# Seven block products in the first feed-forward's way down of a decoder layer

## The chip, the cores and the metric

The kernel runs on one core of one Trainium2 chip. A core has TensorE (PE in the profile; its weight loads are PEld), VectorE (DVE), ScalarE (ACT), GpSimd (POOL) and SyncE (SP), which work on their own queues and wait for each other by semaphores; 16 DMA engines move data between HBM, SBUF and back. The metric is the device time of one execution in microseconds, as the median of the runs; less is better.

## The reference, cut to what matters

One hybrid decoder layer in float32, 1024 tokens of width 1024: a SwiGLU feed-forward, a mixer of stick-breaking attention and a Mamba-2 SSD side by side, a cross-attention to 256 memory tokens, and a second SwiGLU feed-forward, each between two RMS norms. The change is in the first feed-forward's second product.

```python
D_MODEL = 1024
SEQ = 1024
D_FF = 2816

def swiglu(h, w_gu, w_down):
    gu = h @ w_gu
    g, u = jnp.split(gu, 2, axis=-1)
    return (jax.nn.silu(g) * u) @ w_down

def reference(...):
    h = x
    for l in range(DEPTH):
        f = swiglu(rmsnorm(h, ffn1_pre_g[l]), ffn1_w_gu[l], ffn1_w_down[l])
        h = h + 0.5 * rmsnorm(f, ffn1_post_g[l])
        m = hybrid_mixer(rmsnorm(h, mix_pre_g[l]), w_in[l], ...)
        h = h + rmsnorm(m, mix_post_g[l])
        c = memory_cross_attention(rmsnorm(h, xa_pre_g[l]), rmsnorm(mem, mem_g[l]), ...)
        h = h + rmsnorm(c, xa_post_g[l])
        f = swiglu(rmsnorm(h, ffn2_pre_g[l]), ffn2_w_gu[l], ffn2_w_down[l])
        h = h + 0.5 * rmsnorm(f, ffn2_post_g[l])
    return h
```

## The kernel before, in words

**Products.** A float32 product is made of three matmuls in a 32-bit matmul type. Each operand is split into hi, a rounded copy (`split`, L248, an ACT copy), and lo, the remainder (L250, a VectorE subtract); `mm3` issues hi x hi, hi x lo and lo x hi into one PSUM bank. All matmuls pass line 137. Activations are kept transposed: width on the 128 partitions, tokens along a row, in two halves `hh` of H = 512 tokens.

**Seven products for eight.** A product of matrices cut into 2 x 2 blocks needs eight block products, or seven, if sums and differences of the blocks are formed first and the results are combined afterwards. The up phases of both feed-forwards (`seven`) and the second feed-forward's way down (`down7`, called by `down_rows`) are written so. The first one's way down (`down1`) takes all eight: 22 k-tiles of 128, 8 output tiles, 2 halves.

**The first feed-forward.** `ffn1` runs `up_phase`, which for each of 22 tiles f of the inner width makes two activation tiles (one for each half), stores them to HBM (`store`, on ACT's queue) as `act_d`, and then `down1`. `down1` goes in three groups of blocks (0 to 2, 3 and 4, then 5 to 10, where a block is two k-tiles), each for both output halves `dh` and both token halves; between groups the partial sums go from PSUM into `F` (copies L972, sums L477). The last group runs token half 0 first, and `post(0)`, the norm behind the feed-forward of half 0 with its residual and the next norm's scale, runs beside the products of half 1. `post(1)` runs beside the start of the SSD. `post` takes the sums of squares (`sumsq`), two small products that gather them and spread them over the partitions (`rms_cols`, `rms_rows`), then for each of 8 tiles: scale (L388), residual (L392), the hi copy (L399), the lo part (L404) and the next sum of squares (L349, L350). `resid` loads the residual on POOL's queue.

**The second feed-forward's way down.** In `down7` the seven products are `m` = 0 to 6, each over 11 block pairs `j`. For a step (m, j) `fetch` loads the blocks that don't stay in SBUF, forms the weights' sum on VectorE (L1025), splits weights and activations, and `take` keeps some five steps ready ahead. The activations' sums were formed at the end of the up phase (`pair_sums`, or `act_sums`, which reloads the first pairs from HBM) and stored as `xs_d`. Two of the four weight blocks stay in SBUF (`stay`), in the tiles of the normed input that the up phase has done with. In the last product the last four pairs are taken together, bank by bank.

**Order.** TensorE's order is that of the program text. `self.clock` counts the estimated time of TensorE's instructions, 0.422 ns a column; `self.later` holds pairs of such a time and a function, and `run_later` issues what is due after each matmul. Instructions issued that way keep their order on their engines (`kp`). Others are placed by the scheduler.

**Prepared weights.** `prepare_all` splits 58 weight tiles of later stages during the up phase and the way down: each tile in two pieces, a load, a copy (L209), a subtract (L214) and two stores to HBM on SP's queue. Later stages then load hi and lo (L180) and split nothing. Its pieces use SBUF tiles in three places, among them the ninth buffers of `xl0` and `xl1`.

Of the kernel before, what the change touches and what calls it, by code (L numbers as in the profile page):

```python
# [46 lines left out]
class Kern:  # L47
    def __init__(self, nc, tc, ap):
        self.nc, self.tc, self.ap = nc, tc, ap
        self.uid = 0  # L50
        self.clock = 0.0
        self.prev = None
        self.floating = None
        self.pins = []
        self.later = []
        self.inlater = False
        self.more = False
# [131 lines left out]
    def prepare(self, tiles, sp, t0, step):  # L189
# [3 lines left out]
        work, out = [], []  # L193
        for src in tiles:
            hl = tuple(self.tc.dram_tile([P, KT, P], F32R, name=self.nm(n)) for n in ("dwhi", "dwlo"))
            out.append(hl)
            work += [(src, hl, slice(4 * i, 4 * i + 4)) for i in range(2)]
        pools = ((self.fp, "acc0"), (self.fp, "acc1")), ((self.fp, "rpost"), (self.tp, "dg")), ((sp, "bh"), (sp, "bl"))
        raws, his, los = {}, {}, {}

        def load(n):
            pool, tag = ((sp, "braw"), (sp, "braw"), (self.xp, "xl0"), (self.xp, "xl1"))[n % 4]
            raws[n] = self.t(pool, [P, 4, P], F32, tag, bufs=2 if pool is sp else KT + 1)
            self.kp(nc.sync.dma_start(out=raws[n], in_=work[n][0][:, work[n][2], :]))

        def high(n):
            pool, tag = pools[n % 3][0]
            his[n] = self.t(pool, [P, 4, P], F32R, tag)
            self.kp(nc.scalar.copy(his[n], raws[n]))  # L209

        def low(n):
            pool, tag = pools[n % 3][1]
            los[n] = self.t(pool, [P, 4, P], F32R, tag)
            self.kp(nc.vector.tensor_tensor(out=los[n], in0=raws[n], in1=his[n].bitcast(F32), op=ALU.subtract))  # L214

        def store(n):
            for d, x in zip(work[n][1], (his.pop(n), los.pop(n))):
# [288 lines left out]
    def ffn1(self, wgu, wdn, gpre, gpost, gnext, begin):  # L506
# [3 lines left out]
        rw, dnp = st.enter_context(self.pools("ff", [], ["r"]))  # L510
        self.fp = rw
        act_d, bank, load = self.ffn(dnp, rw)
        with tc.tile_pool(name=self.nm("up"), bufs=1, reuse_waits="tile") as sp, \
                tc.tile_pool(name=self.nm("ub"), bufs=1, reuse_waits="tile") as sp2:
            self.up_phase(sp, sp2, wgu, gpre, act_d, bank, load, None, (3, 2, 3), rw, begin)
        f1 = st.enter_context(tc.tile_pool(name=self.nm("d1"), bufs=1, reuse_waits="tile", side="right"))
        with tc.tile_pool(name=self.nm("dl"), bufs=1, reuse_waits="tile") as sp, \
                tc.tile_pool(name=self.nm("d0"), bufs=1, reuse_waits="tile", side="right") as f0:
            self.new_F(f0, f1)
            self.down1(sp, wdn, act_d, bank, load, gpost, gnext)  # L520
# [16 lines left out]
    def up_phase(self, sp, sp2, wgu, gpre, act_d, bank, load, plain, sizes, rw=None, begin=None):  # L537
# [4 lines left out]
        ftp = sp if begin else rw  # L542
# [24 lines left out]
        spare = [] if begin else [self.xl(hh, F32) for hh in range(2)]  # L567

        def store(f, hh, t):
# [3 lines left out]
            if stored[f // 2] == 4 and not begin:  # L573
                later_sums.append(f // 2)

        def act_sums(j, t0):
# [4 lines left out]
            def load(n):  # L581
                if n == "a22":
                    x[n] = self.t(self.tp, [P, H], F32, "dg", bufs=1)
                else:
                    x[n] = self.t(rw, [P, H], F32, "cb", bufs=3)
# [25 lines left out]
        def pair_sums(f, even, odd):  # L611
# [9 lines left out]
            def fresh(n, a, b, op):  # L621
                combine(n, self.t(rw, [P, H], F32, "cb", bufs=3), a, b, op)
# [132 lines left out]
        def seven(f):  # L755
# [40 lines left out]
            if begin or f < 4:  # L796
# [81 lines left out]
    def down1(self, sp, wdn, act_d, bank, load, gpost, gnext):  # L878

        nc = self.nc
        NB = NFF // 2
        dx = [self.t(sp, [P, 2, H], F32R, "dx", bufs=2) for _ in range(2)]
        ends = range(NB - 6, NB)
        groups = [(bs, dh, hh) for bs in (range(0, 3), range(3, 5)) for dh in range(2) for hh in range(2)]
        groups += [(ends, dh, hh) for hh in range(2) for dh in range(2)]
        steps = [(n, b) for n, (bs, _, _) in enumerate(groups) for b in bs]

        def keys(n, b):  # L890
            bs, dh, hh = groups[n]
            return ("a", b, hh), ("w", b, dh, hh if bs is ends else 0)

        uses = {}
        for i, x in enumerate(steps):
            for k in keys(*x):
                uses.setdefault(k, []).append(i)

        spots = {("a", 0, 0): (1, 4), ("a", 1, 0): (1, 6), ("a", 2, 0): (0, 4), ("a", 0, 1): (0, 6), ("a", 1, 1): (1, 0), ("a", 2, 1): (1, 2)}
        for hh in range(2):  # L900
            spots.update({("a", ends[j], hh): (1, k) for j, k in enumerate((4, 6, 0, 2))})

        free, rings = {}, {"a": [], "w": []}
        for k in uses:
            ring = rings[k[0]]
            if k in spots:
                owners = [x for x in uses if spots.get(x) == spots[k] and uses[x][0] < uses[k][0]]
                free[k] = uses[owners[-1]][-1] + 1 if owners else 0
            else:
                free[k] = uses[ring[-4]][-1] + 1 if len(ring) > 3 else 0  # L910
                ring.append(k)
        at, count = {}, [0] * len(steps)
        for k in reversed(list(uses)):
            due = max(uses[k][0] - 2, 0)
# [1455 lines left out]
```

## Time and profile before

| | us |
|---|---|
| median of 3 runs | 2669.76 |
| lowest, highest run | 2667.02, 2671.39 |
| profiled execution | 2668.63 |
| its span, first to last instruction | 2666.4 |
| VectorE busy | 1912.6 |
| ScalarE busy | 1274.6 |
| first up phase, from the span's start to its last product | 452.45 |

The mean granted clock of TensorE is 0.995. In the page, a line of groups reads: line, engine, operation, output <- inputs, count | busy us, mean ns of one | idle time of the engine just before, and who ended it. "x12" behind a timeline's row counts equal instructions in a run. `hl`, `dx`, `whi`, `wlo`, `blk` are buffers of split operands, `dn` and `mm` are PSUM banks.

### The profile page before, as it was taken

How to read it: one execution, taken by the hardware profiler on the slowest of the kernel's cores; microseconds unless marked ns; L12 is line 12 of the kernel's file. 1: busy time of each engine (PE TensorE's matmuls, PEld its weight loads, DVE VectorE, ACT ScalarE, POOL GpSimd, SP SyncE). 2: the span in 40 equal slices, each digit the busy share in tenths (PEclk: the TensorE clock that was granted, in tenths of full speed). 3: DMA queues.
4: the chain of work that ended last, by engine and by line, in shares of the span. 5: the costliest groups of instructions: out<-in, count | busy, mean ns of one | idle time of the engine just before them, and what ended most of it. 6: DMA issues, size and time to landing. Idle time of an engine off the chain costs nothing. (4 is left out here: it accounts for less than half of the span.)

```text
span 2666.4 us, 36628 instructions
## 1 busy us (share of the span) xinstructions
PE 2615.6 (98%) x12970; PEld 2176.7 (82%) x12970; DVE 1912.6 (72%) x2907; ACT 1274.6 (48%) x2263; POOL 591.9 (22%) x676
## 2 busy tenths in 40 slices
PE   9999999999999999999999999999999899999999
PEld 7788888878877778888888897787878688888887
DVE  6888887456568775677777877775557788777777
ACT  7444444444345564555555555354555433333553
POOL 2555553000100000111111110101012655552000
PEclk9999999999999999999999999999999999999999
DMA  5578888984632215444444556544257353236554
GB/s 208 195 267 284 277 284 279 342 288 161 214 127 80 80 64 194 126 122 112 103 121 127 166 164 219 185 150 143 95 177 265 119 166 126 88 107 222 189 168 152
DMA packets 198535, 463.58 MB, mean 174 GB/s; under 512 B 24144, under 2 KB 32720, under 8 KB 198352
## 3 DMA queue, kind: packets, MB, share of 16 engines
q1 hardware_dynamic: 157888, 366.59, 41.4%
q0 software_dynamic: 22464, 61.88, 7.7%
q10 hardware_dynamic: 18000, 32.78, 3.3%
q8 instruction: 102, 1.67, 0.3%
q14 instruction: 81, 0.66, 0.1%
HBM read 313.04 MB, written 127.14 MB: 165 GB/s over the span
## 5 line engine op out<-in xcount | busy, mean ns | idle before, releaser
L137 PE MATMUL mm<-xh,whi 128*128 128x512 f32 x1364 | 536.5, 404 | 7.7 <-ACT xh L248 2.5
L137 PE MATMUL mm<-xh,wlo 128*128 128x512 f32 x1316 | 504.1, 392 | 0.6 <-ACT xh L248 0.6
L137 PE MATMUL mm<-xl,whi 128*128 128x512 f32 (+1 forms) x1258 | 490.0, 390 | 3.2 <-DVE xl L250 3.0
L137 PEld LDWEIGHTS mm<-xh,whi 128*128 128x128 f32 x1364 | 256.8, 188 | 53.3 <-issue 3.8
L137 PEld LDWEIGHTS mm<-xh,wlo 128*128 128x128 f32 x1316 | 247.5, 188 | 54.9 <-ACT xh L248 1.0
L137 PEld LDWEIGHTS mm<-xl,whi 128*128 128x128 f32 x1258 | 237.7, 189 | 37.3 <-DVE xl L250 4.0
L1763 DVE TENSOR_TENSOR_SCAN nb<-nb,begin 128x128 f32<-128x128 f32 (+7 forms) x128 | 171.8, 1353 | 57.8 <-ACT nb L1759 56.8
L1759 ACT ACTIVATE nb<-z,scale 128x128 f32<-128x128 f32 (+2 forms) x192 | 107.9, 581 | 80.0 <-PE z L137 79.8
L248 ACT CAST whi<-wraw 128x1024 fp32r<-128x1024 f32 (+1 forms) x102 | 93.1, 914 | 94.0 <-PE mm L137 66.8
L137 PE MATMUL dn<-xh,wlo 128*128 128x512 f32 x396 | 136.0, 390 | 1.7 <-DMA wlo<-dwlo 1.7
L250 DVE TENSOR_TENSOR wlo<-wraw,whi 128x1024 fp32r<-128x1024 f32 x70 | 85.5, 1221 | 59.1 <-ACT whi L248 58.8
L137 PE MATMUL dn<-xh,whi 128*128 128x512 f32 x356 | 122.8, 391 | 0.0
L1780 POOL DMA_DIRECT2D mix<-sq x64 | 52.8, 826 | 227.2 <-DVE sq L1778 168.6
L710 POOL TENSOR_TENSOR wc<-wraw,raw 128x512 f32<-128x512 f32 x58 | 84.3, 1454 | 74.8 <-DVE whi L250 26.7
L710 POOL TENSOR_TENSOR wc<-raw,wraw 128x512 f32<-128x512 f32 x56 | 83.0, 1481 | 60.9 <-DVE wlo L250 21.4
L795 POOL TENSOR_TENSOR ft<-ft,e 128x512 f32<-128x512 f32 x38 | 62.3, 1640 | 133.5 <-DVE e L794 54.9
L250 DVE TENSOR_TENSOR atl<-tr,ath 128x512 fp32r<-128x512 f32 (+1 forms) x108 | 67.9, 632 | 31.7 <-ACT ath L248 31.2
L632 ACT ACTIVATE ft<-ft 128x512 f32<-128x512 f32 x88 | 55.4, 631 | 73.4 <-DVE ft L631 72.6
L137 PE MATMUL dn<-xh,blk 128*128 128x512 f32 x280 | 90.3, 389 | 0.0
L137 PEld LDWEIGHTS dn<-xh,wlo 128*128 128x128 f32 x396 | 74.4, 188 | 17.9 <-DMA wlo<-dwlo 2.2
L248 ACT CAST whi<-wc 128x512 fp32r<-128x512 f32 x81 | 50.4, 622 | 76.8 <-PE dn L137 30.2
L248 ACT CAST ath<-tr 128x512 fp32r<-128x512 f32 (+1 forms) x108 | 58.9, 546 | 56.5 <-PE tr L140 51.7
(543 smaller groups left out, 6658.1 us busy)
## 6 DMA issues: line engine op xcount, KB each, us to landing
whi<-dwhi SPq DMA_DIRECT2D x78, 512.0 KB, 3.3
wlo<-dwlo SPq DMA_DIRECT2D x78, 512.0 KB, 4.3
wraw<-in_w_gu SPq DMA_DIRECT2D x44, 512.0 KB, 4.0
raw<-in_w_gu SPq DMA_DIRECT2D x38, 512.0 KB, 4.2
act<-ft ACTq DMA_DIRECT2D x70, 256.0 KB, 2.8
h<-F POOLq DMA_DIRECT2D x40, 256.0 KB, 3.0
xl<-h POOLq DMA_DIRECT2D x40, 256.0 KB, 5.2
dwhi<-acc SPq DMA_DIRECT2D x39, 256.0 KB, 5.2
```

Source lines behind the costliest of these rows:

```text
L137: self._pe(self.nc.tensor.matmul(out, lhsT, rhs, start=start, stop=stop, skip_group_check=self.more), cost)
L248: self.kp(self.nc.scalar.copy(hi, src))
L250: self.nc.vector.tensor_tensor(out=lo, in0=src, in1=hi.bitcast(F32), op=ALU.subtract)
L632: nc.scalar.activation(t, t, AF.Silu)
L710: nc.gpsimd.tensor_tensor(out=t, in0=a, in1=b, op=op)
L795: nc.gpsimd.tensor_tensor(out=t1, in0=t1, in1=e, op=ALU.mult)
L1759: nc.scalar.activation(nb[:, s0:s1], z[:, 0:n], AF.Sigmoid, scale=sc[:, i : i + 1])
L1763: nc.vector.tensor_tensor_scan(out=nb[:, 0:Wd][:, ::-1], data0=nb[:, 0:Wd][:, ::-1], data1=begin[:, S - Wd : S][:, ::-1], initial=0.0, op0 ...
L1780: nc.gpsimd.dma_start(out=self.mix_d[p][a * 64 : a * 64 + 64, csl], in_=o, accum_op=ALU.add)
```

## The change

`down1` is rewritten on top of `down7`, which gets a switch: with `rows=False` the weights' tiles are the stationary operand and the activations the moving one, so the result comes transposed, and the blocks of the result are found at other places of `F`. The first up phase forms the activations' sums as the second does: for the last nine pairs from the tiles that are still in SBUF, for the first two by a reload. It gets a pool of its own for that (`up_pool`: six tiles `ft`, three `cb`), which stays open through the way down; four tiles of `F` and the weights' sums then use it. Only 44 weight tiles are prepared in the first feed-forward, at a slower step; the eight `out` tiles are prepared in attention and the six `gu2` tiles in cross-attention, each with a small pool of its own. A prepared piece now uses one of two places, and its four steps are issued at times of their own.

```diff
-    def prepare(self, tiles, sp, t0, step):
+    def prepare(self, names, raw, pairs, t0, step, slow=None):
...
-        def event(n):
-
-            for f, m in ((low, n - 1), (store, n - 2), (high, n), (load, n + 2)):
-                if 0 <= m < len(work):
-                    f(m)
-
-        self.later += [(t0 + step * n, lambda n=n: event(n)) for n in range(-2, len(work) + 2)]
-        return out
+        t = t0
+        for n in range(len(work)):
+            for f, m, dt in ((high, n, 0), (low, n, 1200), (load, n + 2, 2400), (store, n, 3000)):
+                if m < len(work):
+                    self.later.append((t + dt, lambda f=f, m=m: f(m)))
+            t += step if slow is None or t < slow[0] else slow[1]
+        for n in range(2):
+            self.later.append((t0 - 8000 + 1000 * n, lambda n=n: load(n)))
+
+    def prep_pool(self, sp):
+
+        return (sp, "braw"), [((sp, "bh", 2), (sp, "bl", 2)) for _ in range(2)]
 
     def prepare_all(self, sp):
-        ap = self.ap
         names = [("ssd", i) for i in [*range(6), *range(12, 26)]] + [("qkv", i) for i in range(24)]
-        names += [("out", i) for i in range(8, 16)] + [("gu2", i) for i in range(2 * PLAIN)]
-        self.ready = dict(zip(names, self.prepare([ap["w_" + n][i] for n, i in names], sp, 95000, 3870)))
+        pairs = [((self.fp, "acc0", None), (self.fp, "acc1", None)), ((sp, "bh", None), (sp, "bl", None))]
+        self.prepare(names, (sp, "braw"), pairs, 95000, 4700, (418000, 6200))
...
+        self.up_pool = st.enter_context(tc.tile_pool(name=self.nm("uf"), bufs=1, reuse_waits="tile", side="right"))
...
-            self.up_phase(sp, sp2, wgu, gpre, act_d, bank, load, None, (3, 2, 3), rw, begin)
+            xs_d = self.up_phase(sp, sp2, wgu, gpre, act_d, bank, load, None, (6, 2, 3), rw, begin)
...
-            if stored[f // 2] == 4 and not begin:
+            if stored[f // 2] == 4 and f < 4:
                 later_sums.append(f // 2)
...
-            if begin or f < 4:
+            if f < 4:
                 store(f, 0, t0)
                 store(f, 1, t1)
                 return
...
-    def down1(self, sp, wdn, act_d, bank, load, gpost, gnext):
...
+    def down1(self, sp, wdn, act_d, xs_d, gpost, gnext):
+
+        place = self.blocks_down(sp)
+        H_ = [[self.t(self.xp, [P, H], F32, f"xh{hh}{d}") for d in range(KT)] for hh in range(2)]
+        L_ = [[self.xl(hh, F32) for d in range(KT)] for hh in range(2)]
+        stay = {(1, 1): L_[0][4:8] + H_[0][4:8] + H_[0][0:3], (0, 0): H_[1][4:8] + L_[1][4:8] + H_[1][0:3]}
+        accs = []
+
+        def squares(hh, d, tag):
+            if d == 0:
+                accs[:] = self.new_accs(tag)
+            self.sumsq(accs, d, self.F[hh][d])
+
+        def at(t, f, *args):
+            self.later.append((self.clock + t, lambda: f(*args)))
+
+        def finish(m, i):
+            if m == 3:
+                self.run_later(float("inf"))
+                for d in range(4):
+                    at(5000 + 4000 * d, squares, 0, d, "acc0")
+                self.resid(0, 2000, 16000)
+            elif m == 4:
+                self.run_later(float("inf"))
+                for d in range(4, 8):
+                    squares(0, d, "acc0")
+                self.XH[0] = [self.t(self.xp, [P, H], F32R, f"xh0{d}") for d in range(KT)]
+                self.post(0, gpost, self.C[0], gnext, step=2600, accs=accs[:])
+            elif m == 5:
+                for d in range(4):
+                    at(2000 + 4000 * d, squares, 1, d, "bh")
+                self.resid(1, 2000, 14000)
+            elif m == 6:
+                squares(1, 4 + i, "bh")
+
+        self.down7(sp, wdn, act_d, xs_d, place, stay, finish, False)
         self.flush(0)
-        self.post(1, gpost, self.C[1], gnext, step=2000, accs=accs, at=(6500, 9000, 10000), tail=(7500, 10500))
+        self.XH[1] = [self.t(self.xp, [P, H], F32R, f"xh1{d}") for d in range(KT)]
+        self.post(1, gpost, self.C[1], gnext, step=2000, accs=accs[:], at=(6500, 9000, 10000), tail=(7500, 10500))
...
-    def down7(self, sp, wdn, act_d, xs_d, place, stay, finish):
+    def down7(self, sp, wdn, act_d, xs_d, place, stay, finish, rows=True):
...
+                        a, b = (x, w) if rows else (w, x)
                         self.mm3(
-                            banks[i], [(x[:, 0, c], x[:, 1, c], w[:, 0], w[:, 1])], first, j + jj == NB - 1
+                            banks[i], [(a[:, 0, c], a[:, 1, c], b[:, 0], b[:, 1])], first, j + jj == NB - 1
                         )
...
-                    (C11, C12), (C21, C22) = (self.F[hh][2 * i : 2 * i + 2] for hh in range(2))
+                    (C11, C12), (C21, C22) = (
+                        self.F[hh][2 * i : 2 * i + 2] if rows else self.F[hh][i : i + 5 : 4] for hh in range(2)
+                    )
...
+            self.prepare([("out", i) for i in range(8, 16)], *self.prep_pool(wsp), self.clock + 30000, 20000)
...
+                    self.prepare([("gu2", i) for i in range(2 * PLAIN)], *self.prep_pool(wsp), self.clock + 9000, 7000)
```

More of the change, by code (lines that the diff above doesn't have):

```diff
@@ L566, in up_phase @@
         xs_d, stored, later_sums, held = {}, [0] * (NFF // 2), [], []
-        spare = [] if begin else [self.xl(hh, F32) for hh in range(2)]
+        spare = [self.xl(hh, F32) for hh in range(2)]
         def store(f, hh, t):
@@ L876, in up_phase, with blocks_down @@
         return xs_d
[L878 to L883 removed]
+    def blocks_down(self, sp):
         dx = [self.t(sp, [P, 2, H], F32R, "dx", bufs=2) for _ in range(2)]
[L885 to L914, printed above, removed]
[L915 to L921 removed]
+        nblk = [0]
         def place():
```

114 lines of the change are left out of this document (25 added, 89 removed).

## The prediction, made before the changed kernel ran

> **What bounds the kernel now.** I read the page first: engines, then the slices.
>
> ```profile
> span 2666.4 us, 36628 instructions
> PE 2615.6 (98%) x12970; PEld 2176.7 (82%) x12970; DVE 1912.6 (72%) x2907; ACT 1274.6 (48%) x2263; POOL 591.9 (22%) x676
> PEclk9999999999999999999999999999999999999999
> ```
>
> TensorE is busy for 98% of the span at full clock, so it looks like the bound. But matmuls overlap and their ends are modelled, so the price of one is its distance from the next. The chain of waits and TensorE's timeline at both ends of the first way down give it:
>
> ```profile
> 2424.23 138.72 PE dn L137 x612
> ...
> 452.45 0.39 PE L137 MATMUL mm<-xh,whi 128*128 128x512 f32 x1
> ...
> 698.65 0.39 PE L137 MATMUL mm<-xh,whi 128*128 128x512 f32 x1
> ```
>
> 612 matmuls in 138.72 us are 0.2267 us each (the recorded 0.39 is a latency). At 452.45 the last product of the up phase ends and down1 begins; at 698.65 the SSD's first projection begins: 246.2 us. down1 has 22 k-tiles x 8 x 2 halves x 3 = 1056 matmuls, 239.4 us at that pace; the rest is norm products and waits. The waits of TensorE for sums into F, by the view of who waited for whom:
>
> ```profile
> PE mm L137 <- DVE F L477: 1.0, 1, 1.0
> PE dn L137 <- DVE F L477: 0.7, 1, 0.7
> ...
> PE mm L137 <- ACT F L972: 0.5, 1, 0.5
> ```
>
> 2.2 us at changes of accumulation group. So this stage is TensorE's, and a matmul less there is 0.2267 us less. The table of stretches shows how near the others are (length; busy us and count of PE, PEld, DVE, ACT, POOL; clock; DMA share; GB/s):
>
> ```profile
> 180.00:270.00 90.00, 90.00 (x399) 74.55 (x398) 73.60 (x93) 43.08 (x75) 52.74 (x34) 1.00 0.82 271
> 270.00:360.00 90.00, 90.00 (x399) 74.55 (x398) 74.28 (x97) 41.60 (x73) 54.16 (x34) 1.00 0.83 284
> 360.00:450.00 90.00, 90.00 (x399) 74.55 (x398) 69.72 (x91) 41.83 (x76) 42.14 (x27) 1.00 0.80 267
> 450.00:517.00 67.00, 66.46 (x294) 54.72 (x293) 34.17 (x53) 32.41 (x60) 3.81 (x5) 1.00 0.97 349
> 637.00:667.00 30.00, 30.00 (x142) 25.12 (x141) 24.00 (x41) 15.43 (x27) 3.24 (x6) 1.00 0.38 140
> 2448.00:2478.00 30.00, 30.00 (x134) 24.83 (x133) 26.98 (x47) 18.54 (x35) 2.63 (x5) 1.00 0.74 238
> 2478.00:2508.00 30.00, 30.00 (x134) 24.84 (x133) 21.04 (x33) 14.66 (x27) 0.00 (x0) 1.00 0.60 195
> 2598.00:2628.00 30.00, 29.73 (x140) 24.47 (x139) 24.62 (x43) 14.80 (x31) 3.24 (x6) 1.00 0.68 228
> ```
>
> The last three rows are the second feed-forward's way down, which already runs seven products through down7: TensorE loses 0.3 us there, with VectorE at 70 to 90%. VectorE is the next in line, so I price it by its starts:
>
> ```profile
> 2468.57 1.89 DVE L1025 TENSOR_TENSOR wc<-xl,xh 128x512 f32<-128x512 f32 x3
> 2470.38 0.69 DVE L250 TENSOR_TENSOR hl<-wraw,hl 128x512 fp32r<-128x512 f32 x1
> ...
> 2643.29 1.41 DVE L1149 SCALAR_TENSOR_TENSOR F<-F,st,mm 128x512 f32<-128x512 f32 x2 [0.32 <-PE mm L140]
> 2644.61 0.75 DVE L1144 SCALAR_TENSOR_TENSOR F<-F,rh,xl 128x512 f32<-128x512 f32 x1
> ```
>
> Three starts from 2468.57 to 2470.38: 0.60 us for a tensor_tensor of 128x512. Two of the three-operand form from 2643.29 to 2644.61: 0.66.
>
> **The change, part by part.** *TensorE.* Seven products of 11 block pairs, 4 banks, 3 matmuls: 924 for 1056. The two programs' TensorE instructions differ by just these 132; which operand is stationary changes neither count nor shape. 132 x 0.2267 = **-29.9 us**. The old groups' waits go too: **-2.2** (the cover is the other down7, which loses 0.3).
>
> *VectorE in the new way down.* The program's order lists 300 instructions there: 148 subtracts for splits, 55 weight sums, 24 sums into F, 20 subtracts of prepared weights, the rest norms and the last activation sums. At 0.60 that is 181 us under 924 x 0.2267 = 209.5, so on average it is hidden. It isn't spread evenly. post(0) now stands on products six and seven alone. From its first instruction that reads the gathered row to the subtract of the last block pair, VectorE has 68 instructions in order: 16 of the 0.66 form, 52 of 0.60: 41.9 us. They can't begin earlier than the row: post issues it 12.0 us after the fifth product by the kernel's count of 0.216 us a matmul, 12.6 real. The norm products, from the timeline:
>
> ```profile
> 705.69 0.95 PE L137 MATMUL ms<-small,bh 128*128 128x1 f32 x8
> 706.50 0.48 PE L137 MATMUL mm<-xl,whi 128*128 128x512 f32 x1
> ...
> 709.10 1.05 PE L137 MATMUL ms<-ident,cpost 128*128 128x128 f32 x8
> 709.90 0.48 PE L137 MATMUL mm<-xh,whi 128*128 128x512 f32 x1
> ...
> L248 ACT CAST whi<-wraw 128x512 fp32r<-128x512 f32 x15 | 9.3, 621 | 13.2 <-PE mm L137 5.8 <-PE dn L137 4.0 <-DMA wraw<-in_w_dn 3.3
> ```
>
> take 0.8 each (start of the matmul behind less their own): 14.2. With about 0.9 (an estimate: a matmul's latency of some 0.3 and an ACT copy of 0.6, as in the last row) to the row in SBUF: 15.1. So the last subtract ends at 15.1 + 41.9 = 57.0 us or later. TensorE wants it after product six (11 x 2.72 + 1.6 = 31.5), seven steps of product seven (19.0), the next columns' norm product (0.8) and nine matmuls (2.0): 53.4, since down7 takes the last four pairs at once, bank by bank. The rest, three banks, stands behind. So TensorE waits at least 3.7 us. VectorE isn't always ready: 47 instructions in 30 us at 2448 are 0.638 each, 68 of them 43.4 us, 1.5 more; 41 in 30 at 637 are 0.73, 49.8 us, 7.9 more. Ends 3.7 and 11.6; I take **+5.2**, by the 2448 row, as there VectorE is behind with the same function's work. What is late next: the norm product of the columns, which waits for the same queue, so it isn't paid twice.
>
> [...]
>
> [...]
>
> ```profile
> PE ms L137 <- DVE acc L350: 6.5, 2, 6.3
> 1740.00:1850.00 110.00, 103.75 (x523) 87.99 (x522) 74.13 (x163) 56.02 (x108) 14.04 (x26) 0.97 0.44 153
> ```
>
> The longest wait of this trace, 6.3 us, lies in a stretch whose granted clock is 0.97: 3% of 110 us, 3.3. Mine comes in three pieces, one for each of the last pairs, with matmuls between, so I add nothing.
>
> *The up phase.* Nine pairs get five sums on VectorE, two more (the first) eight reloads on POOL's queue and five sums; 37 more stores stand on ACT's queue, behind the sums that they wait for. A pair lasts 2 x 7 x 2.72 = 38.1 us. Five sums: 3.0 us. Prepared pieces fall from one in 3.87 to one in 4.7 us of the kernel's count (0.95 of real): 9.4 to 7.7 a pair, 1.7 x 0.9 = 1.5 less, priced by
>
> ```profile
> L214 DVE TENSOR_TENSOR dg<-braw,rpost 128x512 fp32r<-128x512 f32 x10 | 9.0, 902 | 0.1
> ```
>
> So VectorE goes from 69.72 of 90 to some 73.3 there, and at 73.60 and 74.28 TensorE lost nothing. **+0.5**, bounds 0 and 3 (a wait of the size of those above at each third pair).
>
> *Transfers.* Each step of down7 loads 2 x 256 KB in 2.72 us where neither weights stay: 193 GB/s; a prepared piece (a load and two stores of 256 KB) each 6.5 us: 121. Together 314 in the first two products, under the 349 at which TensorE ran 66.46 of 67 us. Hidden; without that cover it is the second rival.
>
> *The 14 tiles.* 28 pieces: 16 in attention, 20 us apart, 12 in cross-attention, 7 apart. Each is an ACT copy (0.6), a VectorE subtract (0.6 to 0.9) and three issues on SP's queue, where loads of the next weights and of q, k, v stand behind a store that waits for its subtract; those weights are a tile ahead. Attention, by its groups and SP's waits:
>
> ```profile
> L1763 DVE TENSOR_TENSOR_SCAN nb<-nb,begin 128x1024 f32<-128x1024 f32 (+3 forms) x121 | 163.5, 1361 | 55.8 <-ACT nb L1759 54.8
> L1759 ACT ACTIVATE nb<-z,scale 128x384 f32<-128x384 f32 (+2 forms) x180 | 101.1, 581 | 76.8 <-PE z L137 76.5
> SPq L180 <- PE mm L137: 153.5, 27, 8.7
> ```
>
> The scan waits for ACT, ACT for TensorE: both have time over, and SP already waits 153.5 us for TensorE with no harm. **+1**, between 0 and 5 (a sixth of 28 x 1.3 = 36 shows).
>
> Sum: -29.9 - 2.2 + 5.2 + 0.5 + 1.0 = **-25.4**. The profiled execution took 2668.6 (2.2 outside the span): 2643.2. The median of the runs is 2669.8, 1.1 above it: **2644**. By the bounds -28.4 to -12.5: 2641 to 2657.
>
> **Rivals.** *VectorE catches up*: if the order leaves enough ahead of the row, the 5.2 are nothing: -30.6, 2639. For it: the other down7 loses 0.3. Against: the 68 instructions, which that one has not.
>
> *Transfers late in the first two products*: 22 steps and 9 pieces are 18.8 MB; at 284 GB/s (the fullest stretch of the up phase) they take 66.2 us for 59.8: 6.4 more, 2651. Against it: 349 was reached.
>
> *The moved pieces show in attention and cross-attention*: each delays the chain from score to scan by its copy and subtract, 28 x 1.3 = 36 us, for the 1 that I took: 2680, slower. From 0.94 us apiece (26.4 / 28) the gain is gone. For it: TensorE's order is fixed and ACT and VectorE are in order. Against: the idle time above.
>
> *VectorE at 0.90 throughout the new way down*, as L214 beside POOL's sums: 300 x 0.90 = 270 us for 246, 2694; from 0.82 no gain. Against: 0.00 to 3.24 us of POOL in the rows of down7.
>
> That fewer products aren't run is excluded by the 132.
>
> **How the numbers follow.** Forecast 62%, first rival 15, second 14, third 5, fourth 4. A change within 0.2% (5.3 us) can't be told from none. The first three are faster: 90%, leaving one for mixtures; half-exposed pieces end near no change: 4%; slower 6%. The range takes the forecast's own and the first two rivals: **2637 to 2657**; outside lie the last two and the tails, some 15%.
>
> **What would show it.** Between the last up product and the SSD's first projection: 246.2 less some 26, about 220 us. In the last 25 us of it, waits of TensorE for "hl", "dx" or "wlo" of VectorE and for the accumulator of squares, 4 to 12 us in all, and VectorE without idle time. Wrong, if TensorE waits there under 2 us (the first rival) or already in products one to five for transfers (the second); if attention's stretch (1090 to 1600 before) gets longer by over 5 us, the third. If the matmuls' pace leaves 0.2267, the first term falls.

## The result and the profile after

The changed kernel takes 2679.4 us (median of 6 runs, 2678.2 to 2685.2) where the kernel before took 2669.7 in the same session: a ratio of 1.0039, 95% interval 1.0026 to 1.0052. It is slower by some 10 us; 2644 was forecast. Its profiled execution took 2679.0 us with this page (span, engines, clock):

```profile
span 2677.2 us, 36675 instructions
...
PE 2598.9 (97%) x12838; PEld 2158.8 (81%) x12838; DVE 1984.8 (74%) x3051; ACT 1295.3 (48%) x2305; POOL 584.1 (22%) x684
...
PEclk9999999999999999999999999999999999999999
```

The 132 matmuls are gone (12970 to 12838), yet the span grew by 10.8. TensorE's timeline at both ends of the first way down tells where:

```profile
482.95 0.39 PE L138 MATMUL dn<-wlo,whi 128*128 128x512 f32 x1
...
711.07 0.39 PE L138 MATMUL mm<-xh,whi 128*128 128x512 f32 x1
```

| part | before | after | difference | forecast |
|---|---|---|---|---|
| up phase, to the first product of the way down | 452.45 | 482.95 | +30.5 | +0.5 |
| way down | 246.2 | 228.1 | -18.1 | -26.9 |
| from the SSD's first projection to the end | 1967.8 | 1966.2 | -1.6 | +1.0 |

So the way down became shorter, but less than forecast; the later stages lost nothing; and the up phase, which the forecast priced at half a microsecond, took all of the gain and 10 us more. The stretches (length; busy us and count of PE, PEld, DVE, ACT, POOL; clock; DMA share; GB/s):

```profile
180.00:270.00 90.00, 79.08 (x338) 64.06 (x337) 65.07 (x91) 30.97 (x55) 41.40 (x32) 0.98 0.77 265
270.00:360.00 90.00, 83.27 (x347) 67.73 (x346) 68.61 (x93) 37.38 (x67) 45.05 (x30) 0.94 0.69 242
360.00:450.00 90.00, 89.02 (x392) 73.08 (x391) 75.55 (x101) 38.39 (x67) 50.77 (x35) 1.00 0.73 252
...
483.00:513.00 30.00, 30.00 (x133) 24.54 (x131) 22.98 (x36) 15.53 (x29) 4.31 (x6) 1.00 1.04 391
513.00:543.00 30.00, 22.85 (x95) 18.77 (x95) 24.44 (x40) 17.95 (x33) 0.00 (x0) 0.89 0.90 295
...
660.00:711.00 51.00, 49.23 (x218) 40.55 (x218) 46.25 (x77) 25.97 (x45) 8.57 (x16) 0.97 0.60 215
```

Where the kernel before ran TensorE for 90.00 of 90 us, three stretches now lose 10.9, 6.7 and 1.0, and VectorE and ScalarE are *less* busy in the first two of them than before. No engine is short of time there; each waits for another. The waits of TensorE (for whom: us, times, longest), first from 110 us to the end of the up phase, then in the way down:

```profile
PE dn L138 <- DVE e L778: 9.2, 3, 4.8
PE mm L138 <- DVE e L778: 7.6, 3, 4.7
PE mm L138 <- ACT sq L768: 1.8, 1, 1.8
```

```profile
PE dn L138 <- ACT F L1027: 7.1, 1, 7.1
PE ms L138 <- DVE acc L350: 1.8, 1, 1.8
PE dn L138 <- ACT F L1032: 1.7, 1, 1.7
```

18.6 us in the up phase, where the kernel before has none. The clock adds to it: it is granted at 0.50 for 3.4 us from 188.9, 6.8 us from 277.7 and 3.4 us from 322.0. TensorE is busy for 12.4 of these 13.7 us; its matmuls start 0.43 us apart there for 0.23, so by an estimate from these numbers it loses some 6 us. Together some 25 of the 30.5. Of the other 6, some 2.8 are there by 123 us, where the same sum e (L778) comes 2.8 later than before; the rest lies in shorter waits and was not followed.

**Who is late in the up phase.** TensorE waits for the sum e (L778), which empties a bank that TensorE wants next. VectorE makes it from that bank and from d = sq - sq of GpSimd, which needs ScalarE's two copies out of the banks (L768, L772). So the chain begins in ScalarE's queue, and that queue changed. Its waits between 180 and 450 us, before:

```profile
ACT blk L248 <- PE dn L137: 15.3, 11, 2.2
ACT whi L248 <- PE dn L137: 12.3, 9, 2.1
...
ACT rpost L209 <- DMA dwhi<-rpost: 5.8, 4, 3.5
```

and after:

```profile
ACT acc L207 <- DMA dwhi<-acc: 31.3, 14, 4.2
ACT bh L207 <- DMA dwhi<-bh: 31.1, 14, 5.4
...
ACT wlo L248 <- DVE xl L598: 9.1, 1, 9.1
```

Before, ScalarE's casts of weight blocks waited for TensorE, 73.0 us in all (six rows of this kind): it was ahead, and stood until TensorE freed a place. I call that time the up phase's reserve. After, the same casts wait 5.6 us for TensorE, and the preparation's copies wait 62.4 for their own stores (12.0 before), since the high halves have two places where they had three. One place of the reserve's end, in the timeline around the first reload:

```profile
176.64 1.68 POOL L799 TENSOR_TENSOR ft<-ft,e 128x512 f32<-128x512 f32 x1 [1.82 <-DVE e L798]
178.25 1.64 POOL L591 DMA_DIRECT2D cb<-act  x3
...
185.87 1.29 DVE L598 TENSOR_TENSOR xl<-cb,cb 128x512 f32<-128x512 f32 x2 [6.40 <-DMA cb<-act]
187.56 0.62 ACT L248 CAST wlo<-raw 128x512 fp32r<-128x512 f32 x1 [9.09 <-DVE xl L598]
188.28 0.68 DVE L778 TENSOR_TENSOR e<-sq,dn 128x512 f32<-128x512 f32 x1
189.02 2.50 PE L138 MATMUL dn<-S,blk 128*128 128x512 f32 x5 [4.84 <-DVE e L778]
```

The reload is issued on GpSimd's queue behind the last multiplication of the pair; VectorE comes to its sum before the data and stands 6.4 us; the sum e stands behind it; ScalarE stands 9.1 us at the store of that sum; and TensorE loses 4.8.

### The profile page after: what moved, and what is told of

It is laid out like the page before. It is cut to its first block, busy times and chain, and to the rows that moved or that the text cites. A ratio compares the mean times of both kernels' runs of the same rounds, so it can differ in the third digit from the quotient of the medians.

```text
span 2677.2 us, 36675 instructions
## 1 busy us (share of the span) xinstructions
PE 2598.9 (97%) x12838; PEld 2158.8 (81%) x12838; DVE 1984.8 (74%) x3051; ACT 1295.3 (48%) x2305; POOL 584.1 (22%) x684
## 5 line engine op out<-in xcount | busy, mean ns | idle before, releaser
L138 PE MATMUL mm<-xh,whi 128*128 128x512 f32 x1288 | 509.1, 405 | 6.8 <-ACT xh L248 2.7
L138 PE MATMUL mm<-xl,whi 128*128 128x512 f32 (+1 forms) x1220 | 475.5, 390 | 4.4 <-DVE xl L250 4.1
L138 PE MATMUL mm<-xh,wlo 128*128 128x512 f32 x1240 | 476.9, 392 | 0.6 <-ACT xh L248 0.6
L138 PEld LDWEIGHTS mm<-xh,whi 128*128 128x128 f32 x1288 | 242.6, 188 | 48.9 <-ACT xh L248 3.8
L138 PEld LDWEIGHTS mm<-xh,wlo 128*128 128x128 f32 x1240 | 233.1, 188 | 51.7 <-ACT xh L248 1.0
L248 ACT CAST whi<-wraw 128x1024 fp32r<-128x1024 f32 (+1 forms) x88 | 84.4, 960 | 76.2 <-PE mm L138 58.3
L138 PE MATMUL dn<-xh,wlo 128*128 128x512 f32 x296 | 101.3, 390 | 0.3 <-DMA wlo<-dwlo 0.3
L138 PE MATMUL dn<-xh,whi 128*128 128x512 f32 x256 | 88.5, 391 | 0.0
L138 PE MATMUL mm<-ath,v 128*128 128x256 f32 x320 | 85.7, 291 | 0.3
L138 PE MATMUL mm<-atl,v 128*128 128x256 f32 x320 | 82.8, 281 | 0.7 <-DVE atl L250 0.7
```

Of the source, the lines that this page charges most:

```text
L138: self._pe(self.nc.tensor.matmul(out, lhsT, rhs, start=start, stop=stop, skip_group_check=self.more), cost)
L248: self.kp(self.nc.scalar.copy(hi, src))
```

## The experiments

One table first; the times of the parts are from each profile, the medians and ratios from the runs beside the kernel before, whose median was 2669.7 to 2673.9 us in the five sessions. "Reserve" is the sum of the waits of ScalarE's block casts for TensorE between 180 and 450 us. Runs 1, 6, 9, 10 and 15 leave work out, so that their output is not the reference's; their times only show what that work cost.

| run | up phase | way down | SSD from | reserve | median us | ratio (95%) |
|---|---|---|---|---|---|---|
| before | 452.5 | 246.2 | 698.7 | 73.0 | 2669.7 | 1 |
| after | 483.0 | 228.1 | 711.1 | 5.6 | 2679.4 | 1.0039 (1.0026 to 1.0052) |
| 1 no sums | 462.5 | 229.9 | 692.3 | 4.7 | 2664.9 | 0.9976 (0.9965 to 0.9987) |
| 2 three places | 475.2 | 228.4 | 703.7 | 13.0 | 2673.5 | 1.0009 (0.9995 to 1.0023) |
| 3 later sums | 481.0 | 228.7 | 709.7 | | 2679.1 | 1.0035 (1.0023 to 1.0047) |
| 4 qkv in attention | 482.4 | 217.2 | 699.7 | | 2675.5 | 1.0014 (1.0001 to 1.0028) |
| 5 earlier reloads | 479.8 | 227.1 | 706.9 | 2.9 | 2683.0 | 1.0037 (1.0021 to 1.0052) |
| 6 = 1 with 2 | 459.8 | 230.9 | 690.6 | 7.2 | 2664.2 | 0.9960 (0.9947 to 0.9973) |
| 7 = 2, 4, 5, slower pieces | 467.3 | 224.6 | 691.9 | | 2667.7 | 0.9983 (0.9968 to 0.9999) |
| 8 = 2, 4, 5, high store first | 467.5 | 216.6 | 684.2 | 13.2 | 2658.3 | 0.9943 (0.9923 to 0.9962) |
| 9 no stores of sums | 474.8 | 231.0 | 705.8 | 12.2 | 2676.7 | 1.0015 (1.0004 to 1.0026) |
| 10 no reloads | 464.2 | 232.3 | 696.5 | 4.4 | 2668.4 | 0.9977 (0.9967 to 0.9988) |
| 11 = 8, later stores | 460.7 | 222.6 | 683.3 | 25.1 | 2654.8 | 0.9930 (0.9909 to 0.9952) |
| 12 = 11, stores on SyncE | 460.4 | 223.6 | 684.0 | | 2656.2 | 0.9938 (0.9922 to 0.9954) |
| 13 = 11, pieces as in 8 | 460.6 | 216.4 | 677.0 | 22.7 | 2653.2 | 0.9926 (0.9912 to 0.9940) |
| 14 reloads moved alone | 476.9 | 233.1 | 709.9 | 2.7 | 2679.2 | 1.0019 (1.0008 to 1.0029) |
| 15 = 13 without reloads | 454.2 | 216.7 | 671.0 | 58.5 | 2644.6 | 0.9892 (0.9873 to 0.9911) |

Each part is read from one profiled execution. How far a part moves by itself shows where the text of the program is the same: the way down of the changed kernel and of runs 2, 3, 5 and 14 took 227.1 to 233.1 us, and the stages from the SSD to the end took 1966.2 to 1974.7 us in the nine kernels that leave them alone. A difference of a few microseconds between the parts of two runs proves little.

**1, no sums.** Both halves of each activation are stored, the way down loads blocks for sums:

```
-            if stored[f // 2] == 4 and f < 4:
+            if stored[f // 2] == 4 and f < 4 and not begin:
...
-            if f < 4:
+            if begin or f < 4:
                 store(f, 0, t0)
...
+            if not rows and k is None:
+                k = (m % 2, j % 2)
```

> Left out: the sums of activations in the first up phase (neither the 10 from reloads nor the 45 from tiles in SBUF, and their stores); both halves of every activation are stored as before the change, and the way down loads other activation blocks in place of the sums, as many transfers as now. The output is not the reference's. In the changed kernel the up phase ends at 482.95 us, 30.5 later than before. Theory P (the preparation of weights with two pairs of places and two raw buffers makes ScalarE wait in order for its stores): the up phase still ends after 475. Theory S (the sums: reloads, and stores on ScalarE's queue that wait for VectorE): it ends by 457 and TensorE's waits between 180 and 480 fall from about 18 us to under 4. Both in halves, as the single waits suggest (about 11 us at 184, 229, 247 and 252 for S, 7.6 at 274, 320 and 362 for P, each with half-clock time behind it): 464 to 472. The way down stays at 228 within 4 us in each.

The up phase ends at 462.5, 1.5 below the band for both in halves: 20.5 of the 30.5 us hang on the sums, more than a half and less than all. 10 remain, with ScalarE's reserve still at 4.7 us.

**2, three places for high halves.**

```
+        pairs.append([pairs[0][0], pairs[1][0], (self.fp, "rpost", None)])
...
+            place[0] = pairs[2][n % 3]
```

> The sums as in the changed kernel; only the high halves of prepared pieces rotate over three places instead of two (the tile rpost, which nothing else uses in the up phase), so that ScalarE's copy waits for a store that is one piece older. Theory P: ScalarE's waits for dwhi stores (68 us between 180 and 480) fall under 15 us and the up phase ends at 470 or sooner, by 457 if this is all. Theory S: it stays at 479 to 485. Both in halves: 468 to 474.

The waits for dwhi stores fall to 0.6 us, as theory P said, but the up phase only to 475.2, just outside the band of "both in halves". ScalarE now waits 48.5 us between 180 and 450 for raw loads (braw): the preparation has a second place where it is late.

**3, later sums.** Reloads begin at even f; their sums come 8 and their stores 12 us later, other stores 4.5 later.

```
-            if later_sums and f > 6 and f % 2:
+            if later_sums and (f > 7 and f % 2 == 0 if begin else f > 6 and f % 2):
...
-                at(t0 + 9000 + 1200 * i, combine, n, out, a, b, op)
-                at(t0 + 12000 + 1200 * i, put, n)
+                w = 8000 if begin else 0
+                at(t0 + 9000 + w + 1200 * i, combine, n, out, a, b, op)
+                at(t0 + 12000 + w + w // 2 + 1200 * i, put, n)
...
-                at(self.clock + 2500, lambda: self.kp(nc.scalar.dma_start(out=xs_d[n, j], in_=out)))
+                at(self.clock + (7000 if begin else 2500), lambda: self.kp(nc.scalar.dma_start(out=xs_d[n, j], in_=out)))
```

> The preparation as in the changed kernel; the sums later: the two sets of reloads begin at an even f (8 and 10) with their sums 17 instead of 9 us and their stores 24 instead of 12 us after the first load, and the stores of the other sums are put on ScalarE's queue 7 instead of 2.5 us after the sum. Theory S: VectorE's wait for reloads (11.2 us) and ScalarE's behind it (9.1 and 6.9) go, the waits of TensorE at 184, 229, 247 and 252 (11 us) go, and the up phase ends at 470 or sooner. Theory P: 479 to 485. Both in halves: 466 to 473.

481.0, by number theory P; but it didn't test what it was meant to. The reloads now stood right behind the sums of the last pair, waited for the same buffers, and VectorE still waited 10.3 us for them. It says nothing on S.

**4, twelve qkv tiles prepared in attention.**

```
-        names = [("ssd", i) for i in [*range(6), *range(12, 26)]] + [("qkv", i) for i in range(24)]
+        names = [("ssd", i) for i in [*range(6), *range(12, 26)]] + [("qkv", i) for i in range(12)]
...
-            self.prepare([("out", i) for i in range(8, 16)], *self.prep_pool(wsp), self.clock + 30000, 20000)
+            self.prepare([("qkv", i) for i in range(12, 24)] + [("out", i) for i in range(8, 16)], *self.prep_pool(wsp), self.clock + 8000, 6000, (self.clock + 150000, 13000))
```

> Twelve of the 24 prepared qkv tiles (24 pieces) are prepared in attention instead, 6 us apart, the out tiles behind them, 13 apart; no prepared piece is left for the way down. Up phase as in the changed kernel up to 400 us (its last waits, at 362, may go). Theory T (transfers: the pieces saturate the queues at the start of the way down): the wait of 7.15 us in product one and the half clock behind it go, the way down takes 216 to 221 us instead of 228.1. Rival (the copy out of the banks stands behind casts that wait for the blocks' own loads): it stays at 226 to 229. Attention (389 us between its first and last third in both kernels, 1090 to 1600) as long within 3 us if 40 pieces are as free there as 16 were; if each piece cost 0.94, 22 us longer.

The way down takes 217.2: theory T. In the changed kernel (timeline at the end of product one) the copy that empties the first bank stands on ScalarE's queue behind a cast for the next product's block, and that waits for its transfer:

```profile
519.01 0.62 ACT L248 CAST hl<-raw 128x512 fp32r<-128x512 f32 x1 [2.46 <-DMA raw<-xs]
519.53 0.59 ACT L1027 ACTIVATE F<-dn 128x512 f32<-128x512 f32 x1
...
520.18 1.22 PE L138 MATMUL dn<-hl,dx 128*128 128x512 f32 x2 [7.15 <-ACT F L1027]
```

Without pieces in this stage (stretches of the fourth run) the share of DMA is 0.72 for 1.04, and TensorE doesn't wait:

```profile
483.00:513.00 30.00, 30.00 (x134) 24.85 (x133) 26.92 (x44) 18.20 (x34) 4.26 (x6) 1.00 0.72 236
513.00:543.00 30.00, 30.00 (x134) 24.82 (x133) 21.55 (x35) 14.71 (x28) 0.00 (x0) 1.00 0.61 193
```

The rival named the right place (the cast ahead of the copy), but it is the pieces that make the cast late. From the SSD's start to the end it took 1973.0 us, 6.8 more than the changed kernel. That is inside the spread of this part given above, so the price of the 24 moved pieces is not resolved; with the 1977.9 of the seventh run, the longest of those with 24 moved, it is at most some 0.5 us each.

**5, earlier reloads**, and the stores of the other sums 4.5 us later.

```
-            if later_sums and f > 6 and f % 2:
-                act_sums(later_sums.pop(0), self.clock)
+            if later_sums and f > 6 and (f % 2 == 0 if begin else f % 2):
+                act_sums(later_sums.pop(0), self.clock + (12000 if begin else 0))
```

> The sums all there; their order changed alone: the two sets of four reloads are issued 7 us before the product at which they were issued (ahead of GpSimd's last multiplication of the pair, behind which they stood), their sums come 12 us behind them instead of 9, and the stores of all other sums stand 7 instead of 2.5 us behind the sum on ScalarE's queue. In the third experiment the reloads fell behind the last pair's sums and waited for their buffers, so VectorE still waited 10.3 us for them. Theory S by order (each wait of TensorE comes from a reload or store that is late for its place in an engine's order): VectorE waits under 2 us for reloads, the waits at 184, 229, 247 and 252 go, and the up phase ends at 463 to 468. Theory S by work (the 55 sums and stores themselves are too much for VectorE and ScalarE beside the preparation, wherever they stand): it ends at 475 or later.

VectorE no longer waits for a reload at all, and the up phase still ends at 479.8, in the band of "S by work". The waits of TensorE moved, to 222 (4.3 us) and 288 (3.2). So one late reload is not the whole cause; whether it is the work, the fifteenth run below decides for the 45 sums from tiles.

**6, no sums and three places.**

> Left out: the sums, as in the first experiment (same loads on the way down; the output is not the reference's); and the high halves of the preparation rotate over three places, as in the second. The first ended the up phase at 462.5, the second at 475.2, the changed kernel at 483.0, the kernel before at 452.5. If sums and places are all there is: 452 to 456, and no wait of TensorE over 1 us between 110 and the end of the phase. If something else (the slower raw loads, the activations' own stores) keeps part of the 10 us that the first experiment left: 459 or later.

459.8: something else keeps 7. ScalarE's waits for raw loads are 60.9 us here, and its reserve is 7.2: it looks as if the preparation's feed takes it, sums or not.

**7 and 8, the repairs together.** 8 has another order on SyncE:

```
-            for f, m, dt in ((high, n, 0), (low, n, 1200), (load, n + 2, 2400), (store, n, 3000)):
+            for f, m, dt in ((high, n, 0), (low, n, 1200), (lambda m: store(m, 0), n, 1800), (load, n + 2, 4000), (lambda m: store(m, 1), n, 4600)):
```

> All repairs at once: reloads earlier and stores of sums later (as in the fifth), three places for high halves (second), twelve qkv tiles prepared in attention (fourth), and with the pieces left the preparation of the up phase every 5.1 instead of 4.7 us. If both S by order and P hold: up phase to 453 to 458, way down 215 to 219, SSD at 669 to 677; attention and the rest 7 us longer than in the changed kernel as in the fourth, so 2645 to 2655, faster than both kernels. If S by work holds: up phase to 468 or later and 2660 or more.

> As the seventh but with the preparation every 4.7 us, and its SyncE issues in another order: the high half's store first, the next raw load and the low half's store 4 to 4.6 us after the copy, so that SyncE doesn't wait for VectorE's subtract ahead of the high half's store (116 us of SyncE's waits between 180 and 480 in the changed kernel are for that). Theory P: ScalarE's waits for stores fall under 5 us and the time is within 3 us of the seventh's, up phase to 453 to 459. If the later raw load is late in its turn (ScalarE waiting for braw): 3 to 8 us more than the seventh.

The seventh is hardly faster than before, the eighth by 0.6%. Their up phases are equal (467.3, 467.5), 9 above what was expected of both; what divides them is the way down, 224.6 to 216.6, and 6.1 us from the SSD to the end, which are inside that part's spread. At 5.1 us apart the pieces last until 489 us, beside the first loads of the way down, and 4.6 us of wait at its first bank are back. That the eighth would be so much the faster was not expected.

**9 and 10, the sums taken apart.** 9 returns ahead of each store of a sum; 10 never enters the reloads:

```
-            if stored[f // 2] == 4 and f < 4:
+            if stored[f // 2] == 4 and f < 4 and not begin:
```

> Left out: the 55 stores of sums on ScalarE's queue alone; reloads and all sums are computed as in the changed kernel, and the way down loads activation blocks in their place, as many transfers as now (the output is not the reference's). No sums at all gave an up phase of 462.5 us, the changed kernel 483.0. Theory SQ (the stores make ScalarE's queue wait for VectorE and GpSimd, and the urgent copies out of the banks wait behind them): 462 to 467. Theory SV (the sums and reload waits on VectorE itself): 476 to 483. Between: both.

> Left out: the two sets of four reloads, their ten sums and stores (the way down loads activation blocks there; the output is not the reference's). The 45 sums of the nine other pairs and their stores stay. The waits of TensorE at 184 and 229 us with the half clock behind them belong to the reloads, 5.0 + 2.1 and some 3.4 to 5 of clock, so the up phase ends at 470 to 476 if these waits are simply gone. Theory W (the engines' orders are so tight that a wait avoided in one place comes up at the next): 478 or later.

Without the stores 8.1 us less: between the two bands, so both. Without the reloads 18.8 us less, more than the 7 to 13 expected from their own waits and clock, though they are ten of 55 sums.

**11 and 12.** Later stores and sums of a pair in 11, and nine instead of twelve qkv tiles left to attention, so six pieces more than in 8 before the SSD; the stores of the 45 sums on SyncE's queue in 12.

```
-            self.later.append((self.clock + 4500, lambda: self.kp(nc.scalar.dma_start(out=o, in_=t))))
+            self.later.append((self.clock + (7500 if begin and f > 3 else 4500), lambda: self.kp(nc.scalar.dma_start(out=o, in_=t))))
...
-            fresh("s6", t1, t0, ALU.subtract)
+            if begin:
+                c += 2500
+                at(c, fresh, "s6", t1, t0, ALU.subtract)
+            else:
+                fresh("s6", t1, t0, ALU.subtract)
```

> The eighth (up phase to 467.5, way down 216.6, 2658), and: activations' stores 7.5 instead of 4.5 us behind the multiplication, the sums of a pair 2.5 us later, so that VectorE and ScalarE don't wait in order for GpSimd's multiplication of the pair; nine instead of twelve qkv tiles prepared in attention, their six pieces more in the up phase. If in-order waits on ScalarE are what is left (10.9 us behind GpSimd, 5.1 behind the sums): up phase to 458 to 463, way down 216 to 219, 2649 to 2655. If not: 467 and 2656 to 2660.

> The eleventh, with the stores of the 45 sums on SyncE's queue in place of ScalarE's. Theory SQ: up phase 2 to 6 us earlier than in the eleventh. Rival: SyncE's queue, which already waits for VectorE's subtracts, delivers raw weights later, and ScalarE waits for them: the same or up to 10 us later.

The later stores give 7 us of up phase, as expected; the way down loses 6 again, as its pieces lasted until its first loads. Which queue issues the stores makes no difference that these traces show (460.7, 460.4): theory SQ, as a matter of the queue alone, finds no support.

**13, 14, 15.** 13 is 11 with the pieces of 8 and the edit below; 14 is the changed kernel with the fifth's reloads and this edit alone; 15 is 11 with the pieces of 8 and without reloads.

```
-                at(t0 + 12000 + w + 1200 * i, put, n)
+                at(t0 + 12000 + w + (4000 if begin else 0) + 1200 * i, put, n)
```

> The eleventh with twelve qkv tiles prepared in attention again (its down phase was 222.6 with a wait of 3.7 us, since its pieces reached into the way down's first loads; the eighth's was 216.6), and the stores of the reloads' sums 7 instead of 3 us behind the sums. Up phase 454 to 459 if the stores' place is what the reloads cost, 459 to 463 if not; way down 216 to 219; attention some 4 us longer than in the changed kernel; 2644 to 2652 in all.

> The changed kernel with the reloads 7 us earlier, their sums 12 us behind them and their stores 7 us behind the sums; nothing else. If loads and stores that are late for their places make the reloads' cost: up phase 464 to 470, as without reloads (464.2). If the tight order turns any such wait into another one: 475 to 483.

> The thirteenth without the reloads and their ten sums (the way down loads activation blocks there; the output is not the reference's). If reloads, places and order are all: up phase 452 to 455, no wait of TensorE over 1 us between 110 and its end. If something else remains: 457 or later.

The thirteenth's up phase of 460.6 is in the band for "not the stores' place", and its 2653.2 us are 1 above what was expected. Moved alone, the reloads' cost stays for the most part: 476.9, with the largest wait now 5.9 us at 265; the tight order makes another wait of most that are avoided. Left out of the loosened kernel, all but 1.8 us come back, and 1.7 of these are there by 99 us. The stretches of the fifteenth run, its one wait of TensorE over 0.5 us from 110 us to the SSD, and two of ScalarE's waits:

```profile
180.00:270.00 90.00, 90.00 (x399) 74.53 (x398) 76.77 (x105) 41.36 (x73) 49.22 (x32) 1.00 0.77 268
270.00:360.00 90.00, 90.00 (x399) 74.53 (x398) 74.99 (x101) 38.62 (x68) 51.02 (x34) 1.00 0.77 261
360.00:450.00 90.00, 90.00 (x399) 74.53 (x398) 69.00 (x94) 38.13 (x67) 42.94 (x28) 1.00 0.76 257
```

```profile
PE ms L138 <- DVE acc L354: 1.8, 1, 1.8
```

```profile
ACT blk L252 <- PE dn L138: 17.9, 12, 2.2
ACT whi L252 <- PE dn L138: 10.0, 7, 2.1
```

45 sums and 64 prepared pieces run there with VectorE *busier* over the three stretches than in either kernel (220.8 us; 217.6 before, 209.2 after), TensorE at 90.00 of 90, and ScalarE waiting for TensorE again (58.5 us in its six rows). So for these sums the load was not too much; the order was. With all 55 sums that is not shown: the thirteenth, with VectorE at 76.48, 78.06 and 73.84 of 90, still ends its up phase 6.4 us later. The account closes: the reloads with their sums, the places, the order of SyncE's and ScalarE's issues and the 24 pieces moved to attention (0.5 us by themselves, run 4) are 28.7 of the 30.5 us. They don't add up singly: all sums give 20.5 and the places 7.7, but both together 23.2 (run 6). Which of the orders gives how much was not divided further. The thirteenth leaves nothing out, and it is faster than both kernels: 0.9926 of before (0.9912 to 0.9940).

The reserve has to be read stretch by stretch, and as a sign, not as a price. The thirteenth's 22.7 us are 2.6, 3.5 and 16.6 in the three stretches of 90 us; TensorE loses 4.4, 1.2 and 0 there. Over the 13 kernels with a reserve in the table, each stretch in which TensorE lost time had 7.0 us of it or less, and the eight with 16 or more lost nothing; but some with under 7 lost nothing either, and how much is lost doesn't follow from it.

## Why the prediction was wrong

**TensorE, -29.9: right.** The way down without late transfers takes 217.2, 216.6, 216.4 and 216.7 us in four runs: 924 matmuls at 0.2267 are 209.5, and the rest is norm products, one wait of some 2 us and, in some, its clock. The old groups' waits, -2.2, went as well.

**The up phase, +0.5 with bounds 0 and 3: the step that failed.** It measured 30.5. The prediction reckoned that VectorE "goes from 69.72 of 90 to some 73.3 there, and at 73.60 and 74.28 TensorE lost nothing". Load was the wrong measure: in the changed kernel TensorE loses most where VectorE is busy for only 65.07 and 68.61 of 90, and in the fifteenth run it loses nothing at 76.77 and 74.99. The prediction named the eight reloads and the 37 stores "behind the sums that they wait for" and set no price on the waits that they bring into the queues, and it priced the thinner preparation as a gain, while that had lost a third of its places and half of its raw buffers: 62.4 us of ScalarE's waits for stores in place of 12.0. In place of load the runs showed engines that wait for one another in their fixed order: 20.5 of the 30.5 us go with the sums, 18.8 with the reloads and their ten sums alone, and 28.7 when the reloads go and the rest is loosened. The trace before had the warning, though not the price: ScalarE's 73 us of waiting for TensorE were the reserve, 27 of each 100 us, and the forecast never asked what the new waits would leave of it.

**Transfers hidden, 0; second rival 6.4: the rival came true in kind.** By the prediction's own sign, a wait in products one to five for transfers, it holds; its size was 11 us, 228.1 against 217.2: the wait of 7.15, 1.7 at another bank, and the clock behind the first (0.89 of 30 us). The forecast took 314 GB/s, the mean over two products, as the need; in the first 30 us the queues ran full at 391 (share 1.04). It also missed the way by which a late transfer reaches TensorE: not by the block itself, but by a cast for it that stands ahead of the copy out of a bank.

**VectorE late at products six and seven, +5.2 (3.7 to 11.6): the instructions right, the loss smaller.** The 68 instructions run without a gap from

```profile
659.28 0.75 DVE L388 SCALAR_TENSOR_TENSOR F<-F,params,rpost 128x512 f32<-128x512 f32 x1
...
700.58 0.67 DVE L250 TENSOR_TENSOR dx<-cb,dx 128x512 fp32r<-128x512 f32 x1
```

to 701.25: 41.97 us for the forecast 41.9. TensorE waits 1.8 us for the accumulator of squares, and the half clock behind it (3.4 us from 697.5, where matmuls start 0.43 us apart for 0.2267) takes some 1.6: 3.4 in all. The forecast had the wait at the last block pairs, and there is none there; it came at the norm product, which the prediction had not wanted to pay twice. That TensorE, set back so far, meets the last subtract in time is argued, not shown; in the thirteenth run, with the same wait and no half clock, it waits 0.4 us for that subtract. By the prediction's own sign, waits under 2 us, this goes to the first rival, but narrowly, and VectorE had not caught up: it has no idle time until 701.8.

**The 14 tiles, +1 (0 to 5): not contradicted.** From the SSD to the end it took 1.6 us less than before, within the spread of that part. The third rival is refuted: its 36 us would stand far outside that spread, and even the seventh run, with 24 pieces more there, takes 10.1 more than before. That its 2680 is close to the 2679.4 measured is chance; the time was lost in the up phase. **The fourth** (VectorE at 0.90, 294 us of way down for 246) is refuted by 228.1.

## What to carry to other kernels

An engine that is busy for half of the time can still have no time to spare: what counts is for whom it waits. If a helper engine waits for the bound engine, that time is the reserve of the stage. List each new in-order wait (a buffer fewer, a store behind a sum, a reload) beside it, stretch by stretch, and look in the trace after for the moment at which the helper waits for its own stores instead. And when an edit takes buffers from a background task, look for the cost where that task shares a queue with urgent work.

## What the hardware showed that was not expected

Behind a pause of 1.77 us TensorE ran at half clock; behind one of 1.75 us it did not. Both are the same wait for the accumulator of squares, in the changed kernel and in the thirteenth run, by timeline and stretch:

```profile
695.98 1.02 PE L138 MATMUL ms<-small,acc 128*128 128x1 f32 x8 [1.77 <-DVE acc L350]
```

```profile
690.00:705.00 15.00, 13.23 (x60) 10.78 (x59) 13.49 (x24) 7.30 (x14) 4.77 (x9) 0.89 0.96 365
```

```profile
662.21 1.02 PE L138 MATMUL ms<-small,acc 128*128 128x1 f32 x8 [1.75 <-DVE acc L354]
```

```profile
655.00:668.00 13.00, 10.74 (x49) 7.90 (x48) 13.00 (x22) 7.89 (x15) 4.78 (x9) 1.00 0.92 343
```

1.77 us, and the clock is 0.89 of 15 us (0.50 for 3.41 us from 697.50, with matmuls 0.43 us apart for 0.23); 1.75 us, and it stays at 1.00. In the fourth run the same wait takes 2.27 us, and the clock is 0.89 of the 16 us around it. So the prediction's "I add nothing" for waits in pieces was no safe reading of the one long wait that it showed. In the up phase after, half clock behind waits of 4.84, 4.74 and 1.99 us cost some 6 us beside the waits themselves.

What divides the two is not shown. In the changed kernel's trace the half clock begins at 188.91, 277.66, 322.03, 516.59 and 697.50 us and lasts 3.41 us or twice that; these times are 26, 13, 57 and 53 times 3.413 us apart. Around the pause, in stretches of that length:

```profile
694.09:697.50 3.41, 1.64 (x12) 1.46 (x12) 3.41 (x6) 2.10 (x4) 2.54 (x5) 1.00 1.01 383
697.50:700.91 3.41, 3.41 (x10) 2.64 (x9) 3.41 (x7) 1.24 (x2) 0.54 (x1) 0.50 1.02 401
```

The first holds the pause, the eight one-column products and some 0.8 us of full ones, at full clock; the next runs at half clock.
